# One PSUM pool for the whole kernel, a new order of the last output blocks, weights asked for one piece ahead, and a reordered tail, in one layer of a hybrid encoder

## The chip, the cores and the metric

The kernel runs on one core of a Trainium2 chip. The metric is the device time of one execution in microseconds (us), and the time given is the median of several runs. The five engines are named as in the profile: PE multiplies matrices, DVE (VectorE) and ACT (ScalarE) work element by element, POOL (GpSimd) does the same more slowly, and SP issues the transfers between HBM and the core's own memory. PE writes to eight banks of PSUM; DVE and ACT read them.

## The reference

One layer on x of shape (1, 1024, 1024) in float32, cut to what matters here:

```
mod = silu(c) @ w_ada + b_ada;  sh1, sc1, gt1, sh2, sc2, gt2 = split(mod, 6)
h = rms_norm(x) * (1 + sc1) + sh1
q, k, v, g, hc, gb, gc = split(h @ w_in, 7)
ret  = silu(g) * norm(chunk_retention(rotary(q), rotary(k), v))
conv = rms_norm(gb * causal_dwconv(gc * hc))
x = x + gt1 * (concat([ret, conv]) @ w_out)            # 1024 x 1024 x 1024
h = rms_norm(x) * (1 + sc2) + sh2
ua, ub = split(causal_dwconv(h @ w_up), 2)             # d_ff = 2816
x = x + gt2 * ((silu(ua) * ub) @ w_down)
out = rms_norm(x)
```

## The kernel before

Every product is made in three matmuls. An operand is split into a high half (`_h`, a cast by ACT) and a low half (`_l`, the rest, a subtraction by DVE), and `mm3` adds high x high, high x low and low x high into one PSUM bank. A piece of weights therefore goes through four stations: SP's request into a raw tile (three of them, shared by all weights), the cast on ACT, the subtraction on DVE, the matmuls on PE. Matmuls keep the order of the program, the other instructions are ordered by a scheduler unless they are pinned.

The kernel's stages, in the order of time:

- The **conv pieces** (lines 845 to 870): twelve pieces of weights, `gc`, `hc` and `gb` for four groups of channels, 48 matmuls each. In each turn of the loop the weights are requested (`w_col_piece`, line 732), then the matmuls are written, then some adaLN work (`ada_step`), then `down_weights`, which loads two blocks of `w_down`, makes sums of them and stores those (`wop`) for later.
- The **output blocks**, `out_mm`: blocks of 128 rows of concat(...) @ `w_out`, in the groups (0, 1, 2), (3, 4, 5) and (6, 7). For each of eight k the weights `wo` are split, and every block of the group gets its six matmuls into `po`. Then `norm2` adds the gated result to x (line 933 on DVE, 934 on POOL or DVE), squares, and scales (938). `norm2_T` transposes a block on PE (`x1T`), modulates it out of PSUM, and splits sums of it into `h2`. The dictionary `after` says behind which k of a later group the transposes of an earlier block stand.
- The **up loop**: 22 slots of seven products each (a scheme of Strassen's kind, into banks X, Y and Z). A product is 12 matmuls. `seed` copies X into Y, and later products add to both. Products 1 and 2 of the first three slots are made ahead of the loop (`up_product(0, 1)` and so on), beside the transposes of blocks 6 and 7; Z_0 is the first product that needs `h2[3]` and the sums `s_0`.
- The **down products**: seven products (1, 6, 2, 5, 7, 4, 3) of 11 steps, 12 matmuls a step. `operands` requests the two halves of a step into an eight-deep `ring` and splits them.
- The **tail**: `final` norms the blocks 4 to 7 and `out_sum` and `out_scale` the blocks 0 to 3, during and behind the last four steps of product 3.

PSUM is given out by three pools in turn: `psum` (two tiles `m` of two banks, four tiles `r` of one), `psum2` from the up loop on (six banks `x`, two `t`) and `psum3` from the down products on (eight banks). A pool is only opened when everything that used the one before has been read.

Of the kernel before, what the change touches and what calls it, by code (L numbers as in the profile page):

```python
# [18 lines left out]
P = 128  # L19
# [51 lines left out]
def layer(ctx: ExitStack, tc: tile.TileContext, a: dict, out: bass.AP):  # L71
# [772 lines left out]

    n_piece = [0]
    for f in range(4):
        pss = []
        for nm, n0 in (("gc", 12), ("hc", 4), ("gb", 8)):
            w = w_col_piece(a["w_feat"], n0 + f, f"w{nm}_{f}")
            ps = m2k(f"p{nm}_{f}")  # L850
            feat_major(w, ps, h1)
            ada_step(2)
            if n_piece[0] < NK:
                down_weights(n_piece[0])
            n_piece[0] += 1
# [52 lines left out]

    def out_mm(tbs, kinds, after):
        ps = {tb: pair_tiles(f"po_{tb}", kind) for tb, kind in zip(tbs, kinds)}  # L910
        for k in range(KT):
            raw = raw_tile(f"wo_{tbs[0]}_{k}")
            nc.sync.dma_start(flat(raw), a["w_out"][k * P : (k + 1) * P, :])
            w = split(raw, f"wo_{tbs[0]}_{k}")
            for tb in tbs:
# [33 lines left out]

    def norm2_T(tb, bank=None):  # L950
        t = xn2[tb]
        s = slice((tb % 4) * P, (tb % 4 + 1) * P)
        t3 = t.rearrange("p (k t) -> p k t", k=KT)
        if tb >= 4:
            u = w4(f"hu_{tb}")
            nc.sync.dma_start(u, h_d[tb - 4])
            u3 = u.rearrange("p (k t) -> p k t", k=KT)
        for q in range(2):
            pt = bank(f"x1T_{tb}_{q}") if bank else r1k(f"x1T_{tb}_{q}")
            for k in range(4):  # L960
                tr(pt[:, hs(k)], t[:, (4 * q + k) * P : (4 * q + k + 1) * P])
# [38 lines left out]
    nc.vector.tensor_copy(fcol, pf[:, : 8 * NF])  # L1000
    ps = out_mm((3, 4, 5), "mmr", {3: lambda: norm2_T(0), 4: lambda: norm2_T(1), 5: lambda: norm2_T(2)})
# [41 lines left out]
    for tb in range(6, 8):  # L1043
        norm2(ps[tb], tb, nc.gpsimd if tb == 6 else nc.vector)
# [10 lines left out]

    def bank_x(name):
# [19 lines left out]
    def up_product(n, p):  # L1076
# [5 lines left out]
        for k in range(4):  # L1082
            c = slice(hf * 512 + k * P, hf * 512 + (k + 1) * P)
            mm3(S[n][bank], (hi[:, c], lo[:, c]), (b[:, 0, k0 + k], b[:, 1, k0 + k]), k == 0 and not more, k == 3, more)

    def seed(n):
        S[n]["Y"] = bank_x(f"Y_{n}")
        if n < N_EARLY:

            mm(S[n]["Y"], S[n]["a"][0][:, 0:P], h2[0][:, 0, 0])  # L1090
        A(S[n]["Y"], S[n]["X"])

# [58 lines left out]
    def up_slots(n):  # L1151
# [70 lines left out]

    up_product(0, 1)
    seed(0)
    up_product(0, 2)
    norm2_T(6, bank_t)
    up_product(1, 1)
    seed(1)
    up_product(1, 2)
    norm2_T(7, bank_t)  # L1230
    up_product(2, 1)
    seed(2)
    up_product(2, 2)
    for tb in range(4, 8):
        t3_split(tb)
    load_a(0)
    load_b(0)
    sum_a(0)
    sum_b(0)
    lo_of(0, "s")  # L1240
    for n in range(NP + 1):
        up_slots(n)
    fg = cst.tile([P, D], F32, tag="row", name="fg", bufs=2)
    nc.sync.dma_start(fg, a["final_g"].partition_broadcast(P))
    gt2 = cst.tile([P, D], F32, tag="row", name="gt2_again", bufs=2)
    nc.sync.dma_start(gt2, gt2_d)
    mlp_pool.__exit__(None, None, None)
    psum2_pool.__exit__(None, None, None)


    down_pool = tc.tile_pool(name="down_pool", bufs=1)
    dp = down_pool.__enter__()
    psum3 = ctx.enter_context(tc.tile_pool(name="psum3", bufs=1, space=PSUM))
    ring = slab.tile([P, 8, 1024], F32, tag="S1", name="ring")
    x1 = slab.tile([P, TB, D], F32, tag="S0", name="x1")
    for tb in range(TB):
        nc.sync.dma_start(x1[:, tb], x1_d[tb])
    n_raw = [0]
    W_AT = {1: (0, 0), 2: (1, 0), 3: (1, 1)}

    def operands(p, j):
        n = n_raw[0]
        n_raw[0] += 1
        raw = flat(raw_tile(f"raw_{p}_{j}")) if n < 3 else ring[:, n % 8]
        nc.sync.dma_start(raw[:, half[0]], a_ops[p, j])
# [17 lines left out]
    def product(p, ps, start):  # L1283
        for j in range(NK):
            op = operands(p, j)
            for i in range(4):
                step_mm(ps, op, j, i, start)

    def banks(name):
        return [psum3.tile([P, 512], F32, tag="d", name=f"{name}_{i}", bufs=8) for i in range(4)]  # L1290

# [14 lines left out]

    pa = banks("pa")
    product(1, pa, True)
    pb = banks("pb")
    for i in range(4):  # L1310
# [8 lines left out]
    product(5, pb, False)  # L1319
    pa = banks("pc")  # L1320
    product(7, pa, True)
# [19 lines left out]
    KB = NK - 4  # L1341
    for j in range(KB):
        op = operands(3, j)
        for i in range(4):
            step_mm(pa, op, j, i, False)
    tail = {j: operands(3, j) for j in range(KB, NK)}
    for tb in range(4, 8):
        final(tb)

    ys, s0 = {}, {}  # L1350
    for tb in range(4):
        ys[tb] = w4(f"y_out_{tb}")
# [3 lines left out]
        pin(nc.vector.tensor_tensor(out=l, in0=l, in1=fg[:, half[0]], op=ALU.mult))  # L1356

    rs = {}

    def out_sum(tb):  # L1360
# [9 lines left out]
        g = x1[:, tb, half[1]]  # L1370
        pin(nc.vector.tensor_tensor(out=g, in0=g, in1=fg[:, half[1]], op=ALU.mult))

    def out_scale(tb):
        y = ys[tb]
        pin(nc.vector.tensor_scalar(out=y[:, half[0]], in0=x1[:, tb, half[0]], scalar1=rs[tb], scalar2=None, op0=ALU.mult))
        pin(nc.scalar.activation(y[:, half[1]], x1[:, tb, half[1]], AF.Copy, scale=rs[tb]))
        for c in half:
# [65 lines left out]
```

## Time and profile before

| what | value |
| --- | --- |
| time, median of 3 runs | 1185.08 us (1184.3 to 1187.91) |
| the profiled execution | 1186.36 us, of which the span of instructions is 1184.2 us |
| PE busy | 1118.7 us, 94% of the span |
| DVE, ACT, POOL busy | 819.0, 504.6, 129.2 us |
| mean granted clock of PE | 0.98 |

The profile is one execution, seen by the hardware's profiler. Times are us from the start of the span. A busy PE can still be slow: the granted clock tells whether its matmuls ran at full speed (1.0) or half (0.5). In a timeline the bracket at the end of a line is the idle time of the engine ahead of that instruction and what ended it.

### The profile page before, as it was taken

What the parts mean: (1) busy time and instruction counts of PE and PEld (TensorE: products, weight loads), DVE (VectorE), ACT (ScalarE), POOL (GpSimd) and SP (SyncE); (2) the same over time, 40 slices, a digit from 0 to 9 for tenths busy, and PEclk for the clock granted to TensorE, in tenths of its full rate; (3) what the DMA queues carried; (4) which work ended last, traced back from release to release, by engine and by line L of the source; (5) the groups of instructions that cost most, each with busy time, mean ns of one, the idle gap of its engine ahead of it and who ended that gap; (6) DMA issues with size and microseconds to landing.
All of it is one profiled execution on the core that took longest, in us unless ns stands there. A gap on an engine that the chain in (4) does not pass through costs nothing.

```text
span 1184.2 us, 13766 instructions
## 1 busy us (share of the span) xinstructions
PE 1118.7 (94%) x5095; PEld 922.0 (78%) x5095; DVE 819.0 (69%) x1104; ACT 504.6 (43%) x698; POOL 129.2 (11%) x146
## 2 busy tenths in 40 slices
PE   6999999999999999667999999999999989999995
PEld 5788888888877888546788888888888867888884
DVE  6956577576655576855888887888778855464666
ACT  6760123231112345634464554545454534433453
POOL 3503243100000132200000000000000000000024
PEclk9999999999999999978999999999999998999998
DMA  8631422267777357721423332223223398666543
GB/s 316 258 120 58 143 85 95 76 215 258 258 252 273 120 178 256 267 89 35 134 81 108 124 108 97 98 98 125 98 80 108 122 346 298 194 195 194 168 152 142
DMA packets 76990, 190.15 MB, mean 161 GB/s; under 512 B 8164, under 2 KB 8572, under 8 KB 76924
## 3 DMA queue, kind: packets, MB, share of 16 engines
q1 hardware_dynamic: 76924, 189.28, 46.5%
q8 instruction: 40, 0.66, 0.2%
q14 instruction: 26, 0.21, 0.1%
HBM read 146.52 MB, written 42.73 MB: 160 GB/s over the span
## 4 chain that ended last, share of the span: by engine, by line
PE 68%; DVE 12%; DMA 10%; ACT 3%; POOL 3%; issue 3%; SPq 1%; POOLq 0%; DVEq 0%; ACTq 0%
PE Y L113 15%; PE X L113 10%; PE Z L113 10%; PE pb L113 5%; PE pc L113 5%; PE pa L113 4%; PE pq L113 4%; PE pk L113 4%; PE pv L113 2%; DMA wd<-in_w_down_dram 2%; PE po L113 2%; PE pg L113 2%; POOL xr L934 1%; DMA ada_g<-in_w_ada_dram 1%; DMA ada_sh<-in_w_ada_dram 1%
## 5 line engine op out<-in xcount | busy, mean ns | idle before, releaser
L1275 DVE TENSOR_TENSOR op_l<-ring,op_h 128x1024 fp32r<-128x1024 f32 x74 | 90.1, 1224 | 83.6 <-ACT op_h L1274 81.7
L113 PE MATMUL X<-h,a_h 128*128 128x512 f32 x352 | 113.6, 405 | 25.4 <-DVE t L933 13.6
L1274 ACT CAST op_h<-ring 128x1024 fp32r<-128x1024 f32 x74 | 78.0, 1054 | 113.4 <-PE pb L113 36.1
L113 PEld LDWEIGHTS X<-h,a_h 128*128 128x128 f32 x352 | 68.5, 196 | 41.3 <-issue 14.0
L160 POOL TENSOR_SCALAR r<-ss 128x1 f32<-128x1 f32 x20 | 15.6, 778 | 653.3 <-ACT y_out L166 633.2
L113 PE MATMUL po<-wo_h,mix 128*128 128x512 f32 x256 | 82.0, 395 | 0.0
L113 PE MATMUL X<-h,a_l 128*128 128x512 f32 x176 | 70.7, 401 | 0.0
L1018 ACT CAST s_h<-st 128x1024 fp32r<-128x1024 f32 x22 | 23.2, 1053 | 102.7 <-DVE st L1015 102.7
L85 DVE SCALAR_TENSOR_TENSOR act<-ca,fcol,act 128x1023 f32<-128x1023 f32 (+1 forms) x44 | 56.4, 1281 | 1.3 <-ACT act L1116 0.5
L85 DVE SCALAR_TENSOR_TENSOR tb<-cb,fcol,tb 128x1023 f32<-128x1023 f32 (+1 forms) x44 | 56.3, 1280 | 0.7
L113 PE MATMUL Y<-h,b_h 128*128 128x512 f32 x176 | 54.5, 391 | 2.0 <-ACT f L1018 2.0
L113 PEld LDWEIGHTS po<-wo_h,mix 128*128 128x128 f32 x256 | 48.1, 188 | 10.5 <-DVE y L865 0.4
L113 PE MATMUL Z<-h,s_h 128*128 128x512 f32 x176 | 54.2, 389 | 0.0
L113 PE MATMUL Y<-h,s_h 128*128 128x512 f32 x176 | 54.2, 389 | 0.0
L113 PE MATMUL Z<-h,b_h 128*128 128x512 f32 x176 | 54.2, 389 | 0.0
L113 PE MATMUL pb<-op_l,op_h 128*128 128x512 f32 x132 | 51.6, 391 | 2.6 <-DVE op_l L1275 2.6
L113 PE MATMUL pb<-op_h,op_l 128*128 128x512 f32 x132 | 51.4, 389 | 0.0
L113 PE MATMUL pb<-op_h 128*128 128x512 f32 x132 | 51.4, 389 | 0.0
L113 PE MATMUL po<-wo_l,mix 128*128 128x512 f32 x128 | 50.1, 392 | 0.8 <-DVE wo_l L100 0.8
L1015 DVE TENSOR_TENSOR act<-act,tb 128x1024 f32<-128x1024 f32 x22 | 27.0, 1226 | 25.8 <-ACT act L1193 25.5
L99 ACT CAST wo_h<-wo 128x1024 fp32r<-128x1024 f32 x24 | 25.2, 1049 | 38.6 <-PE po L113 17.1
L113 PEld LDWEIGHTS Y<-h,b_h 128*128 128x128 f32 x176 | 32.8, 188 | 10.0 <-ACT f L1018 3.3
(428 smaller groups left out, 3002.9 us busy)
## 6 DMA issues: line engine op xcount, KB each, us to landing
ring<-aop SPq DMA_DIRECT2D x74, 256.0 KB
wa<-in_w_up_dram SPq DMA_DIRECT2D x25, 512.0 KB
wo<-in_w_out_dram SPq DMA_DIRECT2D x24, 512.0 KB
wd<-in_w_down_dram SPq DMA_DIRECT2D x22, 512.0 KB
wb<-in_w_up_dram SPq DMA_DIRECT2D x22, 512.0 KB
aop<-act SPq DMA_DIRECT2D x44, 256.0 KB
ring<-wop SPq DMA_DIRECT2D x44, 256.0 KB
aop<-s SPq DMA_DIRECT2D x33, 256.0 KB
```

What stands on the lines that cost most here:

```text
L85: return nc.vector.scalar_tensor_tensor(out=o, in0=i0, scalar=s, in1=i1, op0=ALU.mult, op1=ALU.add)
L99: c = nc.scalar.copy(hi, src)
L113: pin(nc.tensor.matmul(ps, st, mv, start=start, stop=stop, skip_group_check=more))
L160: q_(nc.gpsimd.tensor_scalar(out=r, in0=ss, scalar1=1.0 / n, scalar2=EPS, op0=ALU.mult, op1=ALU.add))
L934: add.tensor_tensor(out=xt, in0=t, in1=xt, op=ALU.add)
L1015: return pin(nc.vector.tensor_tensor(out=o, in0=i0, in1=i1, op=op))
L1018: return pin(nc.scalar.copy(o, i))
L1274: nc.scalar.copy(hi, raw)
L1275: nc.vector.tensor_tensor(out=lo, in0=raw, in1=hi.bitcast(F32), op=ALU.subtract)
```

## The change

The change has five parts.

1. `psum` stays open to the end. The up loop takes X and Y from the four `r` banks and Z from one half of an `m` tile; the down products take `pa` and `pc` from `m` tiles and `pb` from `r` tiles.
2. The blocks (6, 7) are made with a lag of two: block 7 does its k two steps behind block 6. The transposes of blocks 3, 4 and 5 stand behind steps 1, 3 and 5, `norm2(6)` behind step 7, and `wo` pieces are requested ahead.
3. The early products are ordered X_0, X_1, X_0, x1T_6, X_1, X_2, x1T_7, X_2, and the first halves of X are copied to SBUF (`first_out`); the seeds of slots 0 to 2 move into the slots and copy from there.
4. The weights of a conv piece are requested one turn of the loop ahead (`next_piece`).
5. The first two operands of product 1 are made ahead of the last slot; the eight loads of x1 go out one a step in product 6, which is the second; in product 3 operands, `final` and the left halves of blocks 0 to 3 are interleaved with the steps; in `out_sum` the square's other output goes to `t` and the product with `fg` to `ys`, not in place.

```diff
-    psum_pool = tc.tile_pool(name="psum", bufs=1, space=PSUM)
-    psum = psum_pool.__enter__()
+    psum = ctx.enter_context(tc.tile_pool(name="psum", bufs=1, space=PSUM))
...
+    ahead = next_piece(0)
     for f in range(4):
         pss = []
         for nm, n0 in (("gc", 12), ("hc", 4), ("gb", 8)):
-            w = w_col_piece(a["w_feat"], n0 + f, f"w{nm}_{f}")
+            w, ahead = ahead, next_piece(n_piece + 1)
...
-    def out_mm(tbs, kinds, after):
+    def out_mm(tbs, kinds, after, lag=0):
...
+        for step_ in range(KT + lag * (len(tbs) - 1)):
+            for k in range(step_, step_ + (2 if lag else 3)):
+                piece(k)
+            for n, tb in enumerate(tbs):
+                k = step_ - n * lag
+                if not 0 <= k < KT:
+                    continue
...
-    ps = out_mm((6, 7), "mr", {2: lambda: norm2_T(3), 4: lambda: norm2_T(4), 6: lambda: norm2_T(5)})
+    ps = out_mm(
+        (6, 7), "mm",
+        {1: lambda _: norm2_T(3), 3: lambda _: norm2_T(4), 5: lambda _: norm2_T(5), 7: lambda ps: norm2(ps[6], 6, nc.gpsimd)}, 2,
+    )
...
-        return psum2.tile([P, 512], F32, tag="x", name=name, bufs=6)
+    bank_x = r1k
...
-        return psum2.tile([P, 512], F32, tag="t", name=name, bufs=2)
+        return m2k(name)[:, half[0]]
...
+    def first_out(n):
+        S[n]["p1"] = mlp.tile([P, 512], F32, tag=f"c{n + 1}", name=f"p1_{n}")
+        nc.scalar.copy(S[n]["p1"], S[n]["X"])
...
-        A(S[n]["Y"], S[n]["X"])
+        A(y, S[n]["p1"] if n < N_EARLY else S[n]["X"])
...
-    for tb in range(TB):
-        nc.sync.dma_start(x1[:, tb], x1_d[tb])
...
+            if p == 6 and j < TB:
+                nc.sync.dma_start(x1[:, j], x1_d[j])
...
+    ops3 = {j: operands(3, j) for j in range(4)}
+    for j in range(KB):
+        for i in range(4):
+            step_mm(pa, ops3[j], j, i, False)
+        ops3[j + 4] = operands(3, j + 4)
+        if 2 <= j < 6:
+            final(j + 2)
+        if 3 <= j < 7:
+            left_half(j - 3)
...
-        s1 = square_half(tb, 1, ys[tb][:, half[1]], f"ss3_{tb}_1")
+        s1 = square_half(tb, 1, t, f"ss3_{tb}_1")
...
-        pin(nc.vector.tensor_tensor(out=g, in0=g, in1=fg[:, half[1]], op=ALU.mult))
+        pin(nc.vector.tensor_tensor(out=ys[tb][:, half[1]], in0=g, in1=fg[:, half[1]], op=ALU.mult))
```

In SP's queue before, the weights `wgb_2` of the conv pieces (the ninth of twelve) stand behind the loads `wd` number 7 and ahead of its stores `wop`:

```order
L833 DMA wd_0_7_2894<-in_w_down_dram 128x1024
L833 DMA wd_1_7_2895<-in_w_down_dram 128x1024
L732 DMA wgb_2_2912<-in_w_feat_dram 128x1024
L843 DMA wop_7_7_2248<-tc_7_2898 128x512
L843 DMA wop_5_7_2226<-wd_0_7_2894 128x512
```

In SP's queue of the changed kernel, the same request:

```order
L832 DMA wd_0_6_2822<-in_w_down_dram 128x1024
L832 DMA wd_1_6_2823<-in_w_down_dram 128x1024
L731 DMA wgb_2_2837<-in_w_feat_dram 128x1024
L842 DMA wop_7_6_2247<-tc_6_2826 128x512
L842 DMA wop_5_6_2225<-wd_0_6_2822 128x512
```

It has moved ahead by one whole turn of the loop: it stands behind the loads number 6.

On PE before, the transposes x1T_3 in the last output blocks stand behind the third k (`wo_6_2`) of both blocks:

```order
L113 MATMUL po_7_1_3794<-wo_6_2_l_3834,mix1_2095 128x512
L113 MATMUL po_7_1_3794<-wo_6_2_h_3833,mix1_2095 128x512
L121 MATMUL x1T_3_0_3849<-small_67,t1_3_3755 128x128 x4
L121 MATMUL x1T_3_1_3858<-small_67,t1_3_3755 128x128 x4
L113 MATMUL po_6_3792<-wo_6_3_h_3872,mix1_2095 128x512
```

On PE in the changed kernel, the same transposes:

```order
L113 MATMUL po_6_3792<-wo_6_1_l_3803,mix1_2095 128x512
L113 MATMUL po_6_3792<-wo_6_1_h_3802,mix1_2095 128x512
L121 MATMUL x1T_3_0_3824<-small_67,t1_3_3755 128x128 x4
L121 MATMUL x1T_3_1_3825<-small_67,t1_3_3755 128x128 x4
L113 MATMUL po_6_3792<-wo_6_2_h_3814,mix1_2095 128x512
```

They now stand behind the second k of block 6 alone, with 12 matmuls of these blocks ahead of them where there were 36.

On PE before, the early product X_1 is cut by the matmul that opens the bank Y_1 for its seed:

```order
L113 MATMUL X_1_4205<-h2_0_3200,a_1_h_4026 128x512 x2
L113 MATMUL X_1_4205<-h2_0_3200,a_1_l_4027 128x512
L113 MATMUL Y_1_4218<-h2_0_3200,a_1_h_4026 128x512
L113 MATMUL X_1_4205<-h2_0_3200,a_1_h_4026 128x512 x2
L113 MATMUL X_1_4205<-h2_0_3200,a_1_l_4027 128x512
```

On PE in the changed kernel only Y_0 is opened so, in slot 0, between its first product Z_0 and the next one into Y_0:

```order
L113 MATMUL Z_0_4310<-h2_3_4059,s_0_h_4295 128x512 x2
L113 MATMUL Z_0_4310<-h2_3_4059,s_0_l_4296 128x512
L113 MATMUL Y_0_4326<-h2_0_3200,a_0_h_4032 128x512
L113 MATMUL Y_0_4326<-h2_2_3752,s_0_h_4295 128x512 x2
L113 MATMUL Y_0_4326<-h2_2_3752,s_0_l_4296 128x512
```

The seeds have left the early products; the one of slot 0 now stands between two products of its slot.

## Rows read from the trace of the kernel before

**Rows 1.** waits of PE: line, releaser: us in total, times, longest us.

```profile
PE X L113 <- DVE t L933: 13.6, 1, 13.6
PE X L113 <- ACT Y L1018: 11.8, 3, 5.6
PE pb L113 <- DVE op_l L1275: 2.6, 2, 1.4
```

**Rows 2.** windows: us, busy us (instructions) by engine, clock, DMA share, GB/s.

```profile
495.10:546.70 51.60, 26.21 (x92) 20.34 (x92) 33.53 (x39) 24.38 (x44) 4.47 (x5) 0.74 0.24 82
953.10:991.60 38.50, 33.69 (x135) 26.69 (x134) 22.16 (x20) 16.90 (x18) 0.00 (x0) 0.91 0.99 373
```

**Rows 3.** timeline of PE, conv pieces: start, us, line, out<-in, count, [idle before].

```profile
343.16 0.39 PE L113 MATMUL phc<-hh,whc_l 128*128 128x512 f32 x1
347.05 0.39 PE L113 MATMUL pgb<-hh,wgb_h 128*128 128x512 f32 x1
368.84 0.39 PE L113 MATMUL pgc<-hh,wgc_l 128*128 128x512 f32 x1
375.75 0.39 PE L113 MATMUL phc<-hl,whc_h 128*128 128x512 f32 x1
```

**Rows 4.** timeline of PE, POOL and DVE, last output blocks.

```profile
467.92 0.39 PE L113 MATMUL po<-wo_l,mix 128*128 128x512 f32 x1
475.62 0.39 PE L113 MATMUL po<-wo_h,mix 128*128 128x512 f32 x1
476.73 1.09 PE L121 MATMUL x1T<-small,t 128*128 128x128 f32 x8 [0.72 <-DVE t L938]
473.72 2.40 POOL L934 TENSOR_TENSOR xr<-t,xr 128x1024 f32<-128x1024 f32 x1
473.79 2.88 DVE L938 TENSOR_SCALAR t<-xr,r 128x1024 f32<-128x1024 f32 x1 [3.21 <-POOL r L161]
```

**Rows 5.** timeline of SP and DVE, the request and the split of wgb.

```profile
340.81 0.33 SPq L732 DMA_DIRECT2D wgb<-in_w_feat_dram  x1
345.43 1.23 DVE L100 TENSOR_TENSOR wgb_l<-wgb,wgb_h 128x1024 fp32r<-128x1024 f32 x1 [0.37 <-ACT wgb_h L99]
```

**Rows 6.** line 732 on SP: xcount: duration ns, first and last start us.

```profile
L732 SPq DMA_DIRECT2D wgb<-in_w_feat_dram x4: 327/328/328, 252.0 to 372.3; - x4
```

**Rows 7.** timeline of ACT, POOL and DVE, blocks 4 to 6.

```profile
485.81 2.90 ACT L966 ACTIVATE t<-x1T,m 128x128 f32<-128x128 f32 x8
500.97 2.72 POOL L934 TENSOR_TENSOR xr<-t,xr 128x1024 f32<-128x1024 f32 x1 [21.53 <-DVE t L933]
501.45 3.31 DVE L948 TENSOR_TENSOR h<-t,h 128x1024 fp32r<-128x1024 f32 x1
```

**Rows 8.** timeline of PE and DVE, from x1T_7 to Z_0.

```profile
531.93 1.36 PE L121 MATMUL x1T<-small,t 128*128 128x128 f32 x8
541.85 1.22 PE L113 MATMUL X<-h,a_h 128*128 128x512 f32 x2 [5.59 <-ACT Y L1018]
547.19 0.39 PE L113 MATMUL Z<-h,s_l 128*128 128x512 f32 x1
543.22 1.22 DVE L1015 TENSOR_TENSOR s_l<-st,s_h 128x1024 fp32r<-128x1024 f32 x1
```

**Rows 9.** timeline of SP, and a window, first down product.

```profile
950.78 3.71 SPq L1257 DMA_DIRECT2D x<-x_d  x8
975.00:985.00 10.00, 7.34 (x20) 5.53 (x21) 5.39 (x5) 5.23 (x5) 0.00 (x0) 0.66 1.06 392
```

**Rows 10.** timeline of POOL, PE and DVE, the tail.

```profile
1146.13 6.08 POOL L160 TENSOR_SCALAR r<-ss 128x1 f32<-128x1 f32 x1 [633.20 <-ACT y_out L166]
1173.94 0.39 PE L113 MATMUL pb<-op_h,op_l 128*128 128x512 f32 x1
1174.83 0.69 DVE L1371 TENSOR_TENSOR x<-x,fg 128x512 f32<-128x512 f32 x1 [0.79 <-ACT y_out L1304]
1175.86 0.67 DVE L1362 TENSOR_TENSOR f<-pb,gt_again 128x512 f32<-128x512 f32 x1
```

More of the change, by code (lines that the diff above doesn't have):

```diff
@@ L843, in down_weights, with next_piece @@
             nc.sync.dma_start(w_ops[p, j], src)
-    n_piece = [0]
+    pieces = [(f, nm, n0 + f) for f in range(4) for nm, n0 in (("gc", 12), ("hc", 4), ("gb", 8))]
+    def next_piece(i):
+        if i < len(pieces):
+            f, nm, n = pieces[i]
+            return w_col_piece(a["w_feat"], n, f"w{nm}_{f}")
+    n_piece = 0
+    ahead = next_piece(0)
     for f in range(4):
@@ L907, in layer, with piece @@
     h2 = [slab.tile([P, 2, KT, 512], F32R, tag="S1", name="h2_0"), None, None, None]
-    def out_mm(tbs, kinds, after):
+    def out_mm(tbs, kinds, after, lag=0):
         ps = {tb: pair_tiles(f"po_{tb}", kind) for tb, kind in zip(tbs, kinds)}
[L911 to L915, printed above, removed]
+        w = {}
+        def piece(k):
+            if k < KT and k not in w:
+                raw = raw_tile(f"wo_{tbs[0]}_{k}")
+                nc.sync.dma_start(flat(raw), a["w_out"][k * P : (k + 1) * P, :])
+                w[k] = split(raw, f"wo_{tbs[0]}_{k}")
+        for step_ in range(KT + lag * (len(tbs) - 1)):
[5 more added lines that the diff above has]
+                    continue
                 m = mixes[tb // 4]
@@ L957, in norm2_T @@
             u3 = u.rearrange("p (k t) -> p k t", k=KT)
+        if tb < 6:
+            pts = [r1k(f"x1T_{tb}_{q}") for q in range(2)]
+        else:
+            m = m2k(f"x1T_{tb}")
+            pts = [m[:, h] for h in half]
         for q in range(2):
-            pt = bank(f"x1T_{tb}_{q}") if bank else r1k(f"x1T_{tb}_{q}")
             for k in range(4):
-                tr(pt[:, hs(k)], t[:, (4 * q + k) * P : (4 * q + k + 1) * P])
+                tr(pts[q][:, hs(k)], t[:, (4 * q + k) * P : (4 * q + k + 1) * P])
+        for q in range(2):
+            pt = pts[q]
             for i in range(4):
@@ L1042, in layer @@
         lo_of(n, "a", tt)
-    for tb in range(6, 8):
-        norm2(ps[tb], tb, nc.gpsimd if tb == 6 else nc.vector)
+    norm2(ps[7], 7, nc.vector)
     mix_pool.__exit__(None, None, None)
@@ L1173, in up_slots @@
         if now:
-            if not early:
-                seed(n)
+            seed(n)
         if old:
@@ L1221, in up_slots @@
             lo_of(n + 1, "s")
[L1223 to L1255, printed above, removed]
-    for tb in range(TB):
-        nc.sync.dma_start(x1[:, tb], x1_d[tb])
     n_raw = [0]
+    ring = [None]
     W_AT = {1: (0, 0), 2: (1, 0), 3: (1, 1)}
@@ L1276, in operands @@
         return hi, lo
+    up_product(0, 1)
+    first_out(0)
+    up_product(1, 1)
+    first_out(1)
+    up_product(0, 2)
+    norm2_T(6)
+    up_product(1, 2)
+    up_product(2, 1)
+    first_out(2)
+    norm2_T(7)
+    up_product(2, 2)
+    for tb in range(4, 8):
+        t3_split(tb)
+    load_a(0)
+    load_b(0)
+    sum_a(0)
+    sum_b(0)
+    lo_of(0, "s")
+    for n in range(NP):
+        up_slots(n)
+    first_ops = [operands(1, j) for j in range(2)]
+    up_slots(NP)
+    fg = cst.tile([P, D], F32, tag="row", name="fg", bufs=2)
+    nc.sync.dma_start(fg, a["final_g"].partition_broadcast(P))
+    gt2 = cst.tile([P, D], F32, tag="row", name="gt2_again", bufs=2)
+    nc.sync.dma_start(gt2, gt2_d)
+    mlp_pool.__exit__(None, None, None)
+    down_pool = tc.tile_pool(name="down_pool", bufs=1)
+    dp = down_pool.__enter__()
+    ring[0] = slab.tile([P, 8, 1024], F32, tag="S1", name="ring")
+    x1 = slab.tile([P, TB, D], F32, tag="S0", name="x1")
     def step_mm(ps, op, j, i, start):
@@ L1284, in product, with banks_m @@
         for j in range(NK):
-            op = operands(p, j)
+            op = first_ops[j] if p == 1 and j < 2 else operands(p, j)
+            if p == 6 and j < TB:
+                nc.sync.dma_start(x1[:, j], x1_d[j])
             for i in range(4):
                 step_mm(ps, op, j, i, start)
-    def banks(name):
-        return [psum3.tile([P, 512], F32, tag="d", name=f"{name}_{i}", bufs=8) for i in range(4)]
+    def banks_m(name):
+        t = [m2k(f"{name}_{i}") for i in range(2)]
+        return [t[i // 2][:, half[i % 2]] for i in range(4)]
     def four(name):
@@ L1305, in square_half @@
         return ss
-    pa = banks("pa")
+    pa = banks_m("pa")
     product(1, pa, True)
-    pb = banks("pb")
+    pb = [r1k(f"pb_{i}") for i in range(4)]
     for i in range(4):
@@ L1319, in layer @@
     product(5, pb, False)
-    pa = banks("pc")
+    pa = banks_m("pc")
     product(7, pa, True)
@@ L1341, in layer, with left_half @@
     KB = NK - 4
[L1342 to L1348, printed above, removed]
     ys, s0 = {}, {}
-    for tb in range(4):
+    def left_half(tb):
         ys[tb] = w4(f"y_out_{tb}")
@@ L1375, in out_scale @@
         pin(nc.vector.tensor_scalar(out=y[:, half[0]], in0=x1[:, tb, half[0]], scalar1=rs[tb], scalar2=None, op0=ALU.mult))
-        pin(nc.scalar.activation(y[:, half[1]], x1[:, tb, half[1]], AF.Copy, scale=rs[tb]))
+        pin(nc.scalar.activation(y[:, half[1]], y[:, half[1]], AF.Copy, scale=rs[tb]))
         for c in half:
```

31 lines of the change are left out of this document (14 added, 17 removed).

## The prediction

> **What bounds the kernel now.** I read the waits of PE first, then windows by stage, then the timeline at the places where PE stood still. PE is the bound: nearly every stage is one stream of 128x512 matmuls, which at full clock start 0.2265 us apart (the second matmul of the last output blocks starts at 467.92, the 36th at 475.62: 7.70 us for 34 starts [rows 4]; the 12 matmuls of a slot product or of a down step are therefore 2.72 us). The time can only come from places where PE stands or runs at half clock. The waits name them [rows 1]: 13.6 us in one wait for the VectorE product `t` (line 933), 11.8 us in three waits for the seed copies `Y`, 2.6 us at the last down product. The windows show what stands around them [rows 2]: the stretch 495.10 to 546.70 holds 92 instructions on PE, at a granted clock of 0.74; the first down product takes 38.50 us for 135 matmuls that are worth 30.6.
>
> **The conv pieces (requests one piece ahead).** In the timeline PE issues a matmul at 343.16 and is back in step at 347.05, four starts later: 3.89 − 0.91 = 2.98 us lost. From 368.84 to 375.75 there are 11 starts: 6.91 − 2.49 = 4.42 us lost, the last part at half clock [rows 3]. Behind both stands a late request: SP asks for `wgb` at 340.81, PE wants it at 343.39, and its low half is only computed from 345.43 to 346.66, 5.85 us after the request [rows 5]. SP's four `wgb` requests run from 252.0 to 372.3, nine pieces apart, 13.4 us a piece [rows 6], while PE needs 48 x 0.2265 = 10.9 us for one, so the lead runs out. In the new order SP asks one piece earlier, that is some 13.4 us earlier: `wgb_2` at about 327.4, ready at 333.3, ten microseconds before its use. The raw tile it needs is that of the piece before, whose split is by then long done, and the matmuls that free its high half lie two pieces back. Term: **−7.4**; bounds 0 (the requests were not the cause) and −7.4.
>
> **The last output blocks, two steps apart.** Before, x1T_3 stood behind 36 matmuls; now it stands behind 12. Its input is not earlier: the gate is POOL's additions `xr` and the VectorE scaling behind them, which ran from 473.79 to 476.67 beside one more addition of 2.40 [rows 4], and POOL's order is the same in both kernels. So PE, whose first matmul here starts at 467.92 − 0.23 = 467.69, is done with 12 of them at 467.69 + 2.72 + 0.16 = 470.57 and waits until 476.73: 6.16 us in place of 0.72. That is a new wait, and one during which the clock can fall: after 5.6 us of waiting the matmuls from 541.85 to 547.19, 14 starts, took 5.34 us in place of 3.17 [rows 8]. I take +2.6 for it (bounds 0 and twice the 2.17 just found). From x1T_3's end at 477.6 the chain is: 24 matmuls 5.44 + 2.6 and x1T_4 1.2, to 487.0; 24 matmuls 5.44, plus about 2.5 because the split of `wo_6_5` now stands behind the eight evacuations of block 4 on ACT, which take 2.90 [rows 7], to 494.9; x1T_5 1.1; 36 matmuls 8.16 and once more 2.5 behind block 5's evacuations, to 506.7. Before, it was 495.1: this part is 11.6 us *worse* by itself.
>
> What it buys lies behind it. The bank pool no longer changes, so the first product X_0 doesn't wait for the last read of `po`; it waits for the split `a_0_l`, which the VectorE order puts behind `t1_7` and the split of block 5. Here the trace has a warning: that split took 3.31 us from 501.45 while POOL added `xr` from 500.97 to 503.69 [rows 7]; a subtraction of the same shape takes 1.23 elsewhere [rows 5]. In the new order xr_6 falls into this queue again, so I take the slow price once: `a_0_l` at 509.6, with PE starting its high-half matmuls just ahead, at 509.2.
>
> Six products 16.3 and two transposes 2.2 then run without a seed wait, since the seeds come later and copy from SBUF: end at 527.7, x1T_7 done at 525.0. Before, from x1T_7's end (531.93 + 1.36) to the end of the low half of s_0 (543.22 + 1.22 = 544.44) it took 11.2 us [rows 8]; in the new ACT order one copy p1_2 stands in between and block 6's last splits are nearer, and I take 12.85. So Z_0's third matmul, the first with that half, is at 537.85; before 547.19. That is −9.3. Taken off: PE has stood some 8 us, so half clock costs +2.2 as above; the seed of slot 0 stands between two products that it separates, copy and semaphore about 1.1; slots 1 and 2 some 0.4 each. Term: −9.3 + 2.2 + 1.9 = **−5.2**. Bounds: −13 if neither the split waits nor the clock at x1T_3 cost anything, +5 if each of them costs twice as much.
>
> **The rest of the up loop.** X and Y now have four banks in place of six, and Z shares the two-bank tiles. X_n takes the bank of X_(n−2), whose last reader, the copy into `ca`, ran a slot earlier, and Y_n that of Y_(n−2), read at the latest in the slot behind it. So I cost it at nothing; the cover is one whole slot of 19 us (seven products), and if it were gone each slot would stand.
>
> **The first down product.** SP issues eight x1 loads at 950.78, 3.71 us long, ahead of the operands that PE needs; the stretch 975 to 985 moves 392 GB/s at a DMA share of 1.06, and PE is down to 20 matmuls in 10 us at a clock of 0.66 [rows 9]. The new banks are free at once, and the x1 loads go out one per step of the second product. Then the product should take its 30.6 for the same 135 matmuls: **−7.9** [rows 2]. x1 and operands together are 1.05 MB per step of 2.72 us, 386 GB/s over eight steps, which the 392 of the row just covers; operands are asked for up to eight steps (22 us) ahead, so a small shortfall is absorbed. Bounds: −4 (half of it comes back in product 6) and −8.6. The Trainium skill (DMA: Bandwidth & Descriptors, section "Specifications") gives about 358 GB/s as HBM's limit for a core. By that figure the eight steps (8.39 MB) would take 23.4 us instead of 21.8 and the term would be −6.3, if no lead absorbed it; the 392 of the row is above the figure, so here the row decides.
>
> **The tail.** The last matmul starts at 1173.94, ends at 1174.33, and the first VectorE operation on its block comes at 1175.86, because VectorE waits 0.79 for ACT's square before the product with `fg` is written over its input [rows 10]. The new code writes elsewhere: about −1.4. POOL's first operation after a long idle time takes 6.08 us, and its chain holds VectorE and so the last `op_l`, for which PE stands 2.6 us in two waits [rows 1, 10]. `final` is called earlier, but POOL's first operation still needs block 4's sum; I take −0.6 of these 2.6. Term: **−2.0**, bounds −1.4 and −2.9.
>
> **Sum.** −7.4 − 5.2 − 7.9 − 2.0 = −22.5. The profiled execution took 1186.4 us (span 1184.2, 2.2 around it), 1.3 above the median shown: 1163.9 on its own scale, 1162.6 on that of the median. I say 1163.
>
> **The rivals.**
> *The last blocks give nothing.* For it: a new 6.16 us wait is plain in the order, and two splits stand behind evacuations. With that term 0 to +5: 1168 to 1173. Chance 0.27.
> *The last blocks give much more.* If ACT and VectorE slip the wo splits in time and the clock stays up: term −13, 1155. Against it: the x1T_3 wait is nearly certain. Chance 0.13.
> *The conv waits only move.* SP's cadence of 13.4 us a piece remains; if the earlier request delays the `wd` loads or blocks SP on a raw tile, PE waits elsewhere: 1170. Chance 0.08.
> *Slower: banks.* If a slot's first write to X or Y waits for a copy of the slot before, all 22 slots pay. At 22.5 / 22 = 1.02 us per slot the gain is gone; at one product, 2.72, it is +60 − 22.5, or 1222. For it: six banks became four; against it: the order of last reads above. Chance 0.07.
> *No change.* Conv waits move and the last blocks lose more than 10 us: 0.05.
> My own sum within its bounds (1158 to 1168): 0.40.
>
> **How the numbers follow.** A measurement of this kernel tells about 0.3%, some 3.6 us, from no change. All cases but the last two are faster by more: 0.88, with 0.05 for the same and 0.07 slower. The range for 8 in 10 takes in the sum's own, both cases of the last blocks and the moved conv waits: 1150 to 1176.
>
> **What would show it.** The waits for `wgb_h` and `whc_h` are gone; x1T_3 shows a wait near 6 us, po_7's last matmul comes near 507 and Z_0 near 538; the first down product lasts about 30 us with no wait for `op_h`, at clock 1.0; the first operation on the last block starts within 0.3 us of the last matmul. It would be wrong if a wait for X or Y repeats from slot to slot, if DMA shortage turns up in product 6, or if x1T_3's input comes later than 476.7 because POOL's additions run beside other VectorE work.

## The result

Before: 1185.97 us (median of 4 runs, 1184.3 to 1187.91). Changed: 1173.18 us (median of 4, 1172.99 to 1174.77). The ratio is 0.9895 (95% interval 0.9876 to 0.9913): 12.8 us faster, where 22 were forecast; inside the range, and above the forecast by 10 us.

From the page of the changed kernel, its span and the busy times:

```profile
span 1172.5 us, 13772 instructions
...
PE 1119.9 (96%) x5093; PEld 922.7 (79%) x5093; DVE 821.3 (70%) x1104; ACT 506.3 (43%) x701; POOL 129.7 (11%) x146
```

PE works as long as before and stands less. The span is 11.7 us shorter. Where that comes from is read best from landmarks on PE that both programs have. These are PE's groups by tile of the kernel before: count, shortest/median/longest duration in ns, and the start of the first and of the last.

```profile
L113 PE MATMUL pgc<-hh,wgc_h x64: 389/389/792, 252.6 to 368.4; 128*128 128x512 f32 x64
L113 PE MATMUL R<-diag,ones x4: 590/592/595, 409.6 to 410.8; 128*128 128x512 f32 x4
L113 PE MATMUL pb<-op_h x132: 388/389/397, 991.4 to 1173.5; 128*128 128x512 f32 x132
```

The same groups, and that of Z, in the changed kernel:

```profile
L113 PE MATMUL pgc<-hh,wgc_h x64: 389/389/792, 253.9 to 366.7; 128*128 128x512 f32 x64
L113 PE MATMUL R<-diag,ones x4: 590/592/595, 410.9 to 412.2; 128*128 128x512 f32 x4
L113 PE MATMUL Z<-h,s_l x88: 388/389/792, 539.3 to 935.6; 128*128 128x512 f32 x88
L113 PE MATMUL pb<-op_h x132: 388/389/632, 979.4 to 1163.9; 128*128 128x512 f32 x132
```

`pgc` opens the conv pieces; `R` comes some 15 to 20 us behind their end, among the first output blocks; the first `s_l` into Z is Z_0's third matmul (547.19 before [rows 8]); the up loop ends at 953.1 before [rows 2] and at 949.4 in the changed kernel; `pb` opens the second down product; the last matmul starts at 1173.94 [rows 10] and now at 1164.35. The differences of these starts:

| stretch | before | changed | difference | term of the prediction |
| --- | --- | --- | --- | --- |
| start to the first conv matmul | 252.6 | 253.9 | +1.3 | 0 (not touched) |
| conv pieces, to R | 157.0 | 157.0 | 0.0 | −7.4 |
| R to Z_0's third matmul | 137.6 | 128.4 | −9.2 | −9.3 |
| from there to the end of the up loop | 405.9 | 410.1 | +4.2 | +4.1 |
| first down product | 38.3 | 30.0 | −8.3 | −7.9 |
| second to last product | 182.5 | 185.0 | +2.5 | −0.6 |
| last matmul to the end of the span | 10.3 | 8.2 | −2.1 | −1.4 |

The first row moves from profile to profile: over the kernels of this study the first conv matmul starts anywhere from 251.5 to 254.8, in code that is the same in all.

The waits of PE in the changed kernel (line, releaser: us in total, times, longest us):

```profile
PE Z L113 <- ACT s_h L1044: 8.0, 1, 8.0
PE x1T L121 <- DVE t L955: 5.9, 1, 5.9
...
PE po L113 <- DVE y L872: 3.6, 1, 3.6
PE pb L113 <- DVE op_l L1265: 3.3, 2, 2.5
...
PE po L113 <- DVE wo_l L100: 2.3, 2, 1.2
...
PE po L113 <- ACT wo_h L99: 1.5, 2, 0.8
PE phc L113 <- DVE y L872: 1.4, 1, 1.4
PE Y L113 <- ACT Y L1044: 1.1, 3, 0.7
```

Of the waits of [rows 1], that for `t` is gone and that for `Y` has shrunk from 11.8 to 1.1 us, and no wait for a weight of the conv pieces is left. But `Z` and `x1T` have new waits, and `po` and `phc` now wait for `y` (line 872), for which no matmul waited before: a wait has moved. And `pb` waits longer for `op_l`, 3.3 us for 2.6, not shorter.

**The conv pieces.** The timeline of DVE and PE in the changed kernel at the end of the conv pieces:

```profile
388.74 1.23 DVE L100 TENSOR_TENSOR wo_l<-wo,wo_h 128x1024 fp32r<-128x1024 f32 x1 [4.90 <-ACT wo_h L99]
389.88 1.21 DVE L868 TENSOR_TENSOR gc<-gc,phc 128x1024 f32<-128x1024 f32 x1
...
392.47 2.60 DVE L85 SCALAR_TENSOR_TENSOR y<-gc,vcol,y 128x1023 f32<-128x1023 f32 x2 [0.24 <-ACT y L818]
395.18 1.22 DVE L872 TENSOR_TENSOR y<-y,pgb 128x1024 f32<-128x1024 f32 x1
...
391.24 0.47 PE L113 MATMUL po<-wo_h,mix 128*128 128x512 f32 x1 [0.34 <-DVE gc L868]
...
396.45 0.50 PE L113 MATMUL po<-wo_h,mix 128*128 128x512 f32 x1 [3.58 <-DVE y L872]
...
397.62 0.63 PE L113 MATMUL po<-wo_l,mix 128*128 128x512 f32 x1
```

PE ends the conv pieces 4.5 us sooner (the last one is issued at 390.51, before at 395.03) and then stands 3.58 us, after which its matmuls start 0.43 us apart for a while instead of 0.23: half clock, 1.2 GHz. It waits for one of the two `m` tiles, which `y<-y,pgb` frees. That product ends a chain on DVE that begins with `gc<-gc,phc`; its input was complete on PE ten microseconds earlier, but on DVE it stands behind the split of a piece of `w_out`, whose data comes late, and for which DVE itself stands 4.90 us.

**The last output blocks.** The timeline of PE:

```profile
477.87 1.97 PE L121 MATMUL x1T<-small,t 128*128 128x128 f32 x8 [5.95 <-DVE t L955]
...
491.08 0.51 PE L113 MATMUL po<-wo_h,mix 128*128 128x512 f32 x1 [0.76 <-ACT wo_h L99]
492.74 0.68 PE L113 MATMUL po<-wo_l,mix 128*128 128x512 f32 x1 [1.15 <-DVE wo_l L100]
...
509.83 0.39 PE L113 MATMUL po<-wo_h,mix 128*128 128x512 f32 x1
...
537.53 1.22 PE L113 MATMUL Z<-h,s_h 128*128 128x512 f32 x2 [7.99 <-ACT s_h L1044]
539.33 0.79 PE L113 MATMUL Z<-h,s_l 128*128 128x512 f32 x1 [0.57 <-DVE s_l L1041]
```

The wait at x1T_3 is 5.95 us, the splits of `wo` come late twice (the pair at 501.47 and 503.13 is the same again), and PE stands 8 us before Z_0, whose third matmul is at 539.33.

**The first down product.** Two windows of the changed kernel, the first product and the first eight steps of the second (columns as in [rows 2]):

```profile
949.40:979.20 29.80, 29.80 (x133) 24.66 (x133) 21.61 (x20) 16.28 (x17) 0.00 (x0) 1.00 0.98 356
979.20:1001.00 21.80, 21.80 (x98) 18.06 (x97) 9.80 (x8) 9.49 (x11) 0.00 (x0) 1.00 1.02 378
```

PE is busy through both at full clock, where the same product took 38.50 us at 0.91 [rows 2]. The loads of x1 run in the second window, at 378 GB/s, and nobody waits.

**The tail.** The timeline of POOL, DVE and PE in the changed kernel:

```profile
1134.19 6.48 POOL L159 TENSOR_SCALAR r<-ss 128x1 f32<-128x1 f32 x1 [614.59 <-ACT y_out L165]
...
1136.00 4.62 DVE L1265 TENSOR_TENSOR op_l<-ring,op_h 128x1024 fp32r<-128x1024 f32 x4
1141.35 1.28 DVE L1364 SCALAR_TENSOR_TENSOR y_out<-x,r,fg 128x1024 f32<-128x1024 f32 x1 [0.72 <-POOL r L160]
...
1154.22 0.50 PE L113 MATMUL pb<-op_l,op_h 128*128 128x512 f32 x1 [2.50 <-DVE op_l L1265]
...
1164.78 0.69 DVE L1392 TENSOR_TENSOR f<-pb,gt_again 128x512 f32<-128x512 f32 x1 [0.18 <-PE pb L113]
```

The end is as forecast: DVE is on the last block 0.43 us after the last matmul starts, 1.92 before [rows 10]. But POOL's first operation takes 6.48 us and ends at 1140.67, and DVE stands 0.72 us for the chain behind it, with the later splits still to come; PE shows 3.3 us of waits for splits and, behind the longer one, some matmuls at half clock (up to 632 ns for `pb<-op_h` in the groups above, 397 before).

### The profile page after: what moved, and what is told of

Same layout as the page of the kernel before. It is cut to its first block, busy times and chain, and to the rows that moved or that the text cites. A ratio compares the mean times of both kernels' runs of the same rounds, so it can differ in the third digit from the quotient of the medians.

```text
span 1172.5 us, 13772 instructions
## 1 busy us (share of the span) xinstructions
PE 1119.9 (96%) x5093; PEld 922.7 (79%) x5093; DVE 821.3 (70%) x1104; ACT 506.3 (43%) x701; POOL 129.7 (11%) x146
## 4 chain that ended last, share of the span: by engine, by line
PE 78%; DVE 9%; DMA 4%; POOL 3%; ACT 3%; issue 2%; SPq 0%; POOLq 0%; DVEq 0%; ACTq 0%
PE Y L113 15%; PE X L113 10%; PE Z L113 10%; PE pb L113 6%; PE pa L113 5%; PE pc L113 5%; PE pk L113 4%; PE pgc L113 4%; PE pq L113 3%; PE pg L113 3%; PE po L113 3%; PE phc L113 3%; PE pgb L113 3%; PE pv L113 2%; DMA wo<-in_w_out_dram 1%
## 5 line engine op out<-in xcount | busy, mean ns | idle before, releaser
L113 PE MATMUL X<-h,a_h 128*128 128x512 f32 x352 | 108.6, 390 | 0.0
L113 PE MATMUL po<-wo_h,mix 128*128 128x512 f32 x256 | 87.1, 414 | 5.4 <-DVE y L872 3.6
L113 PEld LDWEIGHTS X<-h,a_h 128*128 128x128 f32 x352 | 65.9, 188 | 13.6
L113 PEld LDWEIGHTS po<-wo_h,mix 128*128 128x128 f32 x256 | 51.2, 200 | 18.2 <-DVE y L872 4.0
L113 PE MATMUL po<-wo_l,mix 128*128 128x512 f32 x128 | 52.8, 412 | 2.3 <-DVE wo_l L100 2.3
L113 PEld LDWEIGHTS Z<-h,s_h 128*128 128x128 f32 x176 | 34.0, 194 | 15.4 <-ACT s_h L1044 8.4
```

Source lines behind the costliest of these rows:

```text
L113: pin(nc.tensor.matmul(ps, st, mv, start=start, stop=stop, skip_group_check=more))
```

## The experiments

**Theories.** For the conv pieces: *theory Q* says that the gain was eaten by DVE's queue, as read above; if so, earlier requests bring nothing in any surroundings, and DVE's order alone brings the gain. Against it stands that the changed kernel did gain there and lost it to something else of the change. For the tail: *theory L* says that POOL's first operation is slow because POOL has rested for 600 us; *theory P*, that POOL and DVE shut each other out, so that POOL stands until DVE pauses. For the last output blocks: what the lag and the earlier transposes that came with it cost, and what the new order of the products behind them brings. The kernels below were measured in three groups, each beside runs of the kernel before on the same chip; medians scatter by some 3 us from chip to chip, and so do the starts of the conv pieces, so each is read by its ratio and by the stretch that it touches.

**1. The requests alone, in the kernel before.**

```diff
...
+    ahead = next_piece(0)
...
-            w = w_col_piece(a["w_feat"], n0 + f, f"w{nm}_{f}")
+            w, ahead = ahead, next_piece(n_piece[0] + 1)
```

> The kernel before with one part alone: conv weights requested one piece ahead. Theory Q (the waits for the weights are gone, but VectorE keeps its order: the product of gc and hc of the last group stands behind the split of a w_out piece that lands late, so PSUM tiles come free late and PE waits at the first output blocks): no gain, between -1 and +2 us against before. Theory R (the requests bring what their two waits cost, 7.4 us, and the other parts of the change lose it): 7 us faster, ratio 0.994. Theory D (the stage is bound by the transfers, whatever stands ahead): also no gain, but with PE waiting for weight or w_out halves themselves.

Measured: 1186.04 us (10 runs) against 1187.65, ratio 0.9988 (0.9973 to 1.0003). From the first conv matmul to R: 157.8 us. PE's waits in this kernel:

```profile
PE po L113 <- DVE y L873: 3.6, 1, 3.6
...
PE phc L113 <- DVE y L873: 1.6, 1, 1.6
...
PE po L113 <- DVE gc L869: 1.2, 1, 1.2
```

The same waits take the place of those for the weights, without the rest of the change. Asking earlier brings 1.6 us by the medians, which is not clear of zero, and by the interval at most 3.2 of the 7.4.

**2. The changed kernel with the requests put back.**

```diff
-    ahead = next_piece(0)
...
-            w, ahead = ahead, next_piece(n_piece + 1)
+            w = next_piece(n_piece)
```

> The changed kernel without the earlier requests. Theory Q: the two waits for wgb and whc come back, the waits for y at the first output blocks go; the output blocks start their transposes some 1.4 us earlier than in the changed kernel, and the time is 1172 to 1173, ratio 0.988. Theory R: 7 us slower than the changed kernel, 1180.

Measured: 1173.67 us, ratio 0.9872 (0.9849 to 0.9895); to R 157.2 us. The waits for `wgb_h` (2.7 us) and `whc_l` (1.6) are back, that for `y` is gone, and the time is the same within the intervals. A start of x1T_3 earlier than in the changed kernel was not seen (478.62, with the conv pieces starting 0.9 later); a shift of that size is within the scatter.

**3. The last group's chain ahead of the splits of w_out on DVE.** In the changed kernel, three splits of the first output blocks, casts on ACT and subtractions on DVE, are issued behind the convolution of the last group.

```diff
+                conv_last = conv3(y, t, cmw[:, f : f + 1], cmw[:, 4 + f : 5 + f], cmw[:, 8 + f : 9 + f], cmb[:, f : f + 1])
...
-                w[k] = split(raw, f"wo_{tbs[0]}_{k}")
+                if tbs[0] == 0 and 1 <= k < 4:
+                    with tc.issue_after(conv_last[0].ins), tc.issue_after(conv_last[1].ins):
+                        w[k] = split(raw, f"wo_{tbs[0]}_{k}")
+                else:
+                    w[k] = split(raw, f"wo_{tbs[0]}_{k}")
```

> The changed kernel, in which the splits of w_out pieces 1 to 3 stand behind the last group's conv operations on VectorE and ScalarE. Theory Q: the product of gc and hc starts within 1 us of its matmuls' end instead of 10 us, PE's waits for y at the first output blocks fall from 3.9 us to at most 1, the clock stays up there, and the time falls by 5 to 6 us, to 1167.5, ratio 0.984. Theory D: the wait moves to the halves of wo, and the time stays at 1173.

Measured: 1167.72 us (1165.36 to 1173.38), ratio 0.9838 (0.9808 to 0.9868). DVE and PE in its timeline, and a window (columns as in [rows 2]):

```profile
381.51 1.21 DVE L868 TENSOR_TENSOR gc<-gc,phc 128x1024 f32<-128x1024 f32 x1
...
391.86 0.50 PE L113 MATMUL po<-wo_h,mix 128*128 128x512 f32 x1 [1.95 <-DVE y L872]
390.00:398.00 8.00, 6.14 (x27) 5.11 (x28) 4.16 (x4) 2.77 (x3) 2.40 (x1) 1.00 0.65 199
```

`gc<-gc,phc` runs 8.4 us sooner, 6 us counted from the first conv matmul; the wait falls to 1.95 us, where at most 1 was expected, PE stays at full clock, and the stretch to R is 153.2 us, 3.8 less. Nothing but the order on DVE and ACT was changed, and of the two it was DVE's queue that `gc<-gc,phc` stood in. Theory Q holds; the median fell by 5.5, of which the rest is within the scatter.

**4. One operation on POOL early, so that it is no longer rested.**

```diff
+    early = cst.tile([P, 1], F32, name="pool_early")
+    pin(nc.gpsimd.tensor_scalar(out=early, in0=p7[0][:, 0:1], scalar1=1.0 / D, scalar2=EPS, op0=ALU.mult, op1=ALU.add))
     product(4, pa, False)
```

> The changed kernel with one small POOL operation on a column of p7, some 30 us ahead of the tail. Theory L (POOL's first operation takes 6.5 us because it is the first after 615 us of rest): the extra operation takes the 6 us, the first one of the tail at most 1.3, PE's waits for op_l (3.3 us) and the half clock behind them (1.6 us) shrink, 3 to 5 us faster, 1169. Theory P (POOL stands while VectorE runs operations with two SBUF inputs without a break: the first operation ended 0.05 us behind the end of such a run in both kernels): the tail's first operation still takes 6 us and the time stays at 1173.

Measured: 1172.22 us, ratio 0.9868 (0.984 to 0.9896). POOL and DVE in its timeline:

```profile
1092.99 0.19 POOL L1355 TENSOR_SCALAR pool_early<-p 128x1 f32<-128x1 f32 x1 [579.04 <-DVE p L1352]
1127.67 6.49 POOL L159 TENSOR_SCALAR r<-ss 128x1 f32<-128x1 f32 x1 [34.48 <-ACT y_out L165]
...
1092.22 1.28 DVE L1352 TENSOR_TENSOR p<-pb,p 128x512 f32<-128x512 f32 x2
...
1129.47 4.63 DVE L1265 TENSOR_TENSOR op_l<-ring,op_h 128x1024 fp32r<-128x1024 f32 x4
```

The early operation takes 0.19 us after a rest of 579; the one in the tail is as slow as ever after a rest of 34. Theory L falls. And the slow one ends at 1134.16, just where DVE's run of `op_l` ends, at 1134.10. The early one is done while DVE is busy, inside the second of two instructions `p<-pb,p`, which have one of their inputs in PSUM: that DVE works is not enough to keep POOL out.

**5. Gaps on DVE.** Behind each split of product 3 DVE copies one column out of PSUM; nothing reads the copy.

```diff
+    def dve_gap():
+        pin(nc.vector.tensor_copy(gap, pc0[:, 0:1]))
...
+        ops3[j] = operands(3, j)
+        dve_gap()
```

> The changed kernel with a copy of one PSUM column put behind each split of the last product on VectorE, so that operations with two SBUF inputs no longer follow each other without a break. Theory P (POOL's small operation stands as long as such a run lasts): the tail's first POOL operation takes at most 2 us in place of 6.5, the operations of final come some 4 us earlier, PE's waits for op_l (3.3 us) fall below 1 and the half clock behind them goes: 3 to 5 us faster, 1169. Theory L (the first operation after a rest is slow) has lost its main point already; it would expect 6 us still and 1173.

Measured: 1171.07 us, ratio 0.9874 (0.9851 to 0.9897). POOL and DVE in its timeline:

```profile
1133.44 1.95 POOL L159 TENSOR_SCALAR r<-ss 128x1 f32<-128x1 f32 x1 [614.51 <-ACT y_out L165]
...
1145.79 3.27 POOL L160 TENSOR_TENSOR r<-r,nhalf 128x1 f32<-128x1 f32 x1
...
1135.25 0.15 DVE L1363 COPY gap<-pc 128x1 f32<-128x1 f32 x1
1135.32 1.22 DVE L1265 TENSOR_TENSOR op_l<-ring,op_h 128x1024 fp32r<-128x1024 f32 x1
```

A copy of 0.15 us lets POOL through: 1.95 us instead of 6.48, ending at 1135.39 with the first gap. A later operation, which starts just behind a gap, has to wait for the next one at 1148.58 and takes 3.27. One wait for `op_l` is left, 2.4 us, where less than 1 in all was expected; the half clock behind it is gone, and the products from the second on take 182.1 us, 2.9 less. In the seven other kernels that keep this tail (the changed one and those of experiments 2, 3, 4, 6, 8 and 9) this stretch takes 184.9 or 185.0 us, so the gain is clear there, though the ratio of the whole is not clear of the changed kernel's. Theory P holds. The Trainium skill (SBUF — State Buffer, section "SBUF: two separate sides") says that VectorE and GpSimd share a pair of ports, that a VectorE instruction with two inputs in SBUF holds it for its whole length against a GpSimd operation that reads SBUF, and that the other then stands entirely. The trace agrees, and shows more: the operations ahead of the copy have two inputs in SBUF, and back to back they keep POOL out from one instruction to the next, 6.48 us long.

**6. The transposes of blocks 3 to 5 two steps later, the lag kept.**

```diff
-        {1: lambda _: norm2_T(3), 3: lambda _: norm2_T(4), 5: lambda _: norm2_T(5), 7: lambda ps: norm2(ps[6], 6, nc.gpsimd)}, 2,
+        {3: lambda _: norm2_T(3), 5: lambda _: norm2_T(4), 7: lambda ps: (norm2(ps[6], 6, nc.gpsimd), norm2_T(5))}, 2,
```

> The changed kernel with the transposes of blocks 3, 4 and 5 behind steps 3, 5 and 7 of the last output blocks instead of 1, 3 and 5. My account of the last blocks: x1T_3's wait falls from 5.9 us to under 1, the clock stays up behind it, po_7 ends some 6 to 8 us earlier, and Z_0 starts 3 to 6 us earlier: 1168. Rival V (VectorE's and ScalarE's work between the blocks sets when Z_0 can start, wherever PE waits): the wait only moves to X_0 or Z_0, and the time stays within 1.5 us of 1173.

Measured: 1166.7 us (1166.24 to 1166.84), ratio 0.9829 (0.9813 to 0.9844). PE's groups by tile:

```profile
L113 PE MATMUL R<-diag,ones x4: 590/592/595, 409.4 to 410.7; 128*128 128x512 f32 x4
L113 PE MATMUL Z<-h,s_l x88: 388/389/792, 531.3 to 927.7; 128*128 128x512 f32 x88
```

The transposes now have 36, 60 and 84 matmuls of these blocks ahead of them, as in the kernel before. The wait at x1T_3 is gone; `po` waits 4.3 us for a split and X 2.8 and 1.5, and R to Z_0's third matmul takes 121.9 us instead of 128.4. So most of what the last blocks lost comes back with the lag in place.

**7. The loads of x1 in the second product, alone, in the kernel before.**

```diff
-    for tb in range(TB):
-        nc.sync.dma_start(x1[:, tb], x1_d[tb])
...
+            if p == 6 and j < TB:
+                nc.sync.dma_start(x1[:, j], x1_d[j])
```

> The kernel before with one part alone: the eight loads of x1 go out one a step in the second down product; the three PSUM pools stay. By the sum: the first down product takes 30 us without the waits of 2.9 and 0.5 us and without half clock, 6.8 us faster than before; the pool change's wait of 1.4 us stays: ratio 0.9943. Rival: the loads starve product 6 in turn, and half or more comes back: 3 us faster or less.

Measured: 1180.67 us, ratio 0.9946 (0.9928 to 0.9965). From the first `pa` to the first `pb` it takes 30.1 us; in the kernel before 36.5 (954.9 to 991.4). In this product the waits for operands are gone and that for the bank (1.4 us, for the copy `ca`) stays, as it must with three pools. This part of the change is worth 6 to 7 us by itself.

**8. The changed kernel without the lag.** Blocks 6 and 7 do their k in step, and the transposes have their old number of matmuls ahead of them, as before the change. Without a lag the code also asks for the pieces of `wo` up to two steps ahead instead of one; all else of the change stays.

```diff
-        {1: lambda _: norm2_T(3), 3: lambda _: norm2_T(4), 5: lambda _: norm2_T(5), 7: lambda ps: norm2(ps[6], 6, nc.gpsimd)}, 2,
+        {2: lambda _: norm2_T(3), 4: lambda _: norm2_T(4), 6: lambda _: norm2_T(5), 7: lambda ps: norm2(ps[6], 6, nc.gpsimd)}, 0,
```

> The changed kernel without the lag: blocks 6 and 7 take every k together, the transposes of 3, 4 and 5 stand behind k 2, 4 and 6 as before the change; the one pool, the order of the early products and the late seeds stay. If the lag costs what its waits cost (my account): po_7 ends near 497 instead of 510, X_0 starts near 500 and Z_0 near 529 instead of 539, 8 to 10 us faster than the changed kernel, 1164. Rival V (VectorE's and ScalarE's queues set Z_0): PE waits longer for X_0 or Z_0, and the time is 1171 to 1174.

Measured: 1166.17 us (1164.5 to 1166.75), ratio 0.9826 (0.9807 to 0.9846). PE in its timeline:

```profile
477.05 1.09 PE L121 MATMUL x1T<-small,t 128*128 128x128 f32 x8 [0.73 <-DVE t L955]
...
493.25 0.39 PE L113 MATMUL po<-wo_h,mix 128*128 128x512 f32 x1
...
529.72 0.79 PE L113 MATMUL Z<-h,s_l 128*128 128x512 f32 x1 [0.57 <-DVE s_l L1041]
```

The last `po` is 16.6 us sooner, Z_0's third matmul 9.6 sooner; from R to it 119.9 us. That is only 2 us less than in experiment 6, where the lag stayed, and the times of the two kernels are the same. So it was the early place of the transposes, ahead of their input, that cost 6.5 of the 8.6 us; for the lag itself, and the pieces of `wo` asked for earlier, 2 us remain, and this stretch differs by that much between kernels with the same code there (126.0 to 128.7 in the changed kernel and experiments 2 to 5).

**9. Numbers 3 and 8 together.**

> The changed kernel with two of the edits together: the last conv group's operations ahead of the w_out splits on VectorE and ScalarE, and no lag in the last output blocks. If the two losses are separate places, the gains add: 4 to 6 us and 7 us off 1173, so 1161 to 1163, ratio 0.978. If an earlier start of the output blocks only makes PE wait for the same chain of blocks 3 to 5 (the transposes' inputs), the sum is no better than the no-lag kernel alone, 1166.

Measured: 1162.61 us (5 runs, 1159.28 to 1165.45), ratio 0.9776 (0.9749 to 0.9804). Conv pieces to R 152.7 us, R to Z_0's third matmul 121.0.

**10. Numbers 3, 5 and 8 together,** with one more gap behind each `left_half`.

> The changed kernel with the three edits: conv operations first, no lag, and the one-column copies on VectorE in the last product, one more behind each left half. Expected from the single runs: 1173 - 5 - 7 - 3.5 = 1157.5, ratio 0.975; PE's wait for op_l under 1 us in all, since the power operation that still took 3.3 us has a break behind it now. If POOL's release at the breaks was chance, 1161 as without them.

Measured: 1159.08 us (5 runs, 1156.86 to 1160.37) against 1188.51, ratio 0.9753 (0.9727 to 0.9779): faster than both kernels. What is left of its waits:

```profile
PE Z L113 <- ACT s_h L1048: 7.7, 1, 7.7
...
PE pb L113 <- DVE op_l L1269: 2.1, 1, 2.1
...
PE po L113 <- DVE y L872: 0.4, 1, 0.4
```

POOL's first operation in the tail takes 1.94 us; but one wait for `op_l` of 2.1 us stays, more than expected. Against the changed kernel the conv pieces give 6.9 us (150.1 to R; the same edit gave 3.8 and 4.3 in experiments 3 and 9), the last blocks 8.5 (119.9), the products 3.2 (181.8).

## Why the prediction was off, point by point

**The conv pieces: wrong.** The failed step is "Term: **−7.4**". The waits for weights ended as it said, and the time between the first conv matmul and R did not change by 0.1 us. The step took two stalls for lost time without asking what comes next in the line: PE feeds two `m` tiles that DVE empties, and DVE came no earlier. With DVE's old order, the six kernels with the early requests (the changed one and experiments 1, 4, 5, 6 and 8) show 155.4 to 157.8 us and the three without (before, 2 and 7) 157.0, 157.2 and 160.2: the requests bring at best a little over 1 us on average, within this scatter. The three kernels with the new order on DVE and ACT show 150.1 to 153.2, below all of these (experiments 3, 9 and 10). The rival "the conv waits only move" had the outcome (1170) at a chance of 0.08, but named another cause, the `wd` loads. Those have a part in it: at `phc` the product `y` stands on DVE behind a sum that waits 5.70 us for `wd`, though whether the earlier requests delayed `wd` is not shown; for `po`, the larger wait, it is the split of `w_out`.

**The last output blocks: right, step by step.** x1T_3's wait was put at 6.16 us and was 5.95; Z_0's third matmul was to be 9.3 us sooner and is 9.2; half clock and the seeds in the slots were to give back 4.1 and give back 4.2. What the prediction weighed as one term is two: what comes behind the blocks gains, and the transposes ahead of their input lose 6.5 us of it (128.4 against 121.9 in experiment 6), 8.6 with the lag undone as well (119.9 in experiment 8). The prediction had this in sight, "this part is 11.6 us *worse* by itself", and it is the reason why the rival of −13 wasn't reached.

**The banks: right.** No wait for X or Y repeats from slot to slot; new are only those for the three seeds (1.1 us in all).

**The first down product: right,** −8.3 for −7.9, and −6.4 for the loads alone (experiment 7). The doubt from the Trainium skill's figure (DMA: Bandwidth & Descriptors, section "Specifications", about 358 GB/s from HBM for a core) did not come true: the first eight steps of the second product drew 378 GB/s for 21.8 us and waited for nothing.

**The tail: half wrong.** The end gave 2.1 us for the 1.4 forecast. The failed step is "I take −0.6 of these 2.6": the waits for `op_l` grew from 2.6 to 3.3 us, the longest from 1.4 to 2.5, with half clock behind it, and the products took 2.5 us more. The row with POOL's 6.08 us stood in the profile, and the prediction read it as what follows "a long idle time". It isn't that (experiment 4): DVE shut POOL out (experiment 5). That is not new in this order: before, too, a run on DVE with four splits in it kept POOL out for 6.08 us, and POOL's first operation starts at the same place, 154.8 us behind the start of the second product (154.7 before), though `final` is called earlier. What is new is that the last split starts 0.8 us later, counted from the start of the second product (173.5 us against 172.7); which of the moved operations makes it late was not tried.

**The sum.** 22.5 forecast and 11.7 found in the span: 7.4 of the difference are the conv pieces, 2.4 the tail, 1.3 the later start of the conv pieces, which nothing in the change explains; the other terms differ by 0.4 at most. The time lies inside the range because the range left room for a term of that size to fail, not because the sum held.

**Open.** The 8 us before Z_0 stand in all versions with the new order of early products (6.1 to 8.0 us); the chain through block 7's norm, transposes and sums was not tried. Why one `op_l` wait stays in the last version was not followed up. The gain behind the last blocks is read from the waits that are gone; the one pool, the order of the early products and the late seeds were not tried without each other.

## What to carry to other kernels

Before a stall is booked as a gain, follow the stalled engine's next buffer to the engine that frees it, and look what stands ahead of that in its queue: here the waits for weights hid waits for DVE that cost about as much. A long time for a tiny operation on POOL should be laid beside DVE's row at the same time before anything else is blamed. And a change in parts that the profile separates is worth trying without each of them, one at a time: here the early place of three transposes cost half of what the whole gained, and undoing it together with the lag would have put that down to the lag.

## What the runs showed of the hardware

A 128x1 operation on POOL that took 0.19 us beside a DVE instruction with one input in PSUM (experiment 4) took 6.08 [rows 10], 6.48 and 6.49 us while DVE ran instructions with two inputs in SBUF one behind the other, and ended each time within 0.1 us of the end of that run; a copy of one column out of PSUM, 0.15 us, between them cut it to 1.95. Whether it is the pause or the copy's source that lets POOL in at the copy was not told apart; for the source speaks that the early operation of experiment 4 needed no pause. Behind a wait of 3.58 us on PE the matmuls came at half clock, 0.43 us apart, and behind 1.95 us at the same place (experiment 3) at full. The length of one wait does not tell: in the kernel before, waits of 1.81 and 0.52 us in the stretch of [rows 3] from 368.84 to 375.75 were followed by matmuls 0.43 us apart, and in experiment 5 a wait of 2.36 us for `op_l` was not.
